# Context products of an expert matrix in one batch ahead of the latents' products, with three split buffer pairs and seven raw buffers

## The chip, the cores and the metric

One core of one Trainium2 chip runs the whole program. The metric is the time on the device in microseconds (us) of one launch, the median over runs.

## What is computed

Two layers over 1024 latent tokens and 256 context tokens of 1024 channels. Each layer has a token mixer and then a mixture of 16 experts in which each expert chooses its tokens: an eighth of the tokens per expert, so 128 latents and, in layer 0 alone, 32 context tokens. The part of the reference that the change touches:

```python
def ec_moe(h, router, w_gate, w_up, w_down):
    cap = CAPACITY_FACTOR * n // N_EXPERTS
    aff = jax.nn.softmax((h @ router).astype(jnp.float32), axis=-1)
    g, idx = lax.top_k(jnp.swapaxes(aff, 1, 2), cap)
    xg = jax.vmap(lambda hb, ib: hb[ib])(h, idx)
    a = jnp.einsum('becd,edf->becf', xg, w_gate)
    u = jnp.einsum('becd,edf->becf', xg, w_up)
    y = jnp.einsum('becf,efd->becd', jax.nn.silu(a) * u, w_down) * g[..., None]
...
x = x + g2 * ec_moe(h_l, ...)
if need_ctx:
    ctx = ctx + cg2 * ec_moe(h_c, ...)
```

Latents and context go through the same three 1024 x 1024 matrices of an expert (gate, up, down), each with its own choice of tokens.

## The kernel before

The program goes through the recurrence of layer 0, its experts (from about 550 to 1365 us of the span), the attention of layer 1, its experts (about 1860 to 2425 us) and the final norm. The change lies in the experts of layer 0.

**Weights.** The 48 expert matrices of a layer come as chunks of 1 MB, four to a matrix, [128 partitions, 2048]: two of the 8 steps of the contraction each. `Stream` issues their loads on SP's queue, in the order of use, into as many raw buffers as its pools have: `raw0` has four, and `rawx` adds one in layer 0. `done(i)` gives the buffer of chunk i back, and `fill` issues the next load into it, which waits for the last readers of the buffer.

**Latents.** A chunk is split into a high part `wh` (a copy on ACT, L209) and a low part `wl` (a subtraction on DVE, L210), both read from the raw chunk. `mm3` (L218, L220, L222) makes one step of the contraction out of six matmuls of 128 x 128 stationary by 512 columns: high by high, high by low, low by high, each for two halves of the 1024 columns. Eight steps make one matrix. `split_upto(k)` issues the splits up to chunk k. It is called at every even step, for AHEAD = 3 chunks past the one in use, and four pairs of `wh` and `wl` take turns: three in the pool `wspA`, one in `wspB` (`Ring`).

**Context.** The 32 context tokens use the raw chunk, unsplit, in fp32. `ctx_mm(c)` puts two steps of the contraction by two halves of the columns side by side on the four column groups of the array: four matmuls of 128 x 32 stationary by 512 columns (L1188), in the profile eight, since each is two instructions. I call these eight a context group. There are four groups to a matrix; `matrix` puts one behind every odd step of the latents, and the chunk's raw buffer is free after it. After the fourth group the result leaves by `joined` (a copy on ACT, L1153, an addition on DVE, L1154), and Silu, the product with the up result or `put` follow. In the very last matrix alone (down of expert 15) all four groups run first and `after_ctx` follows at once, since the context's keys and values are made beside its latents.

**Order.** The order is written by hand: gate(e+1), down(e), up(e+1), and so on; at the end up(15), down(14), down(15). Hooks put small work behind a step: transposes of the activations behind steps 2, 3 and 5 of a gate product (`A_AT`), of the next expert's rows behind steps 3, 4 and 5 of an up product (`X_AT`), each through two PSUM buffers `tp`, and the index matmuls `mt` behind step 6 of a gate product. Names in the profile: `acc` and `accc` are the sums of latents and context, `xh`, `xl`, `ah`, `al` the latents' stationary parts, `xc`, `ac` the context's, `yl`, `yc` the weighted results that POOL adds to `xr` and `xc` in memory by an indirect DMA.

In the loop of a matrix the order is this:

```python
for kt in range(KT):
    k = k0 + kt // 2
    if kt % 2 == 0:
        split_upto(k + AHEAD)
    h, lo = sp[k]
    mm3(acc, side[0][:, kt], side[1][:, kt], h[:, kt % 2], lo[:, kt % 2], D, kt == 0, kt == KT - 1)
    if has_ctx and not after_ctx and kt % 2:
        ctx_mm(kt // 2)
```

Of the kernel before, what the change touches and what calls it, by code (L numbers as in the profile page):

```python
# [9 lines left out]
F32 = mybir.dt.float32  # L10
# [4 lines left out]
OP = mybir.AluOpType  # L15
# [22 lines left out]
class Stream:  # L38
    """Weight chunks of 1 MB, loaded in the order of use as far ahead as buffers allow."""
# [17 lines left out]
    def fill(self, gate=None):  # L57
        """gate: an operation on the buffer that the load has to follow."""
# [34 lines left out]
class Ring:  # L93
    """Four buffers of a tag in turn, three in one pool and one in another."""
# [10 lines left out]
class Parts:  # L105
    """Pools side by side, each of its own tags, so that memory is handed on part by part."""
# [14 lines left out]
def hybrid_kernel(ctx: ExitStack, tc: tile.TileContext, I, out, dbg=None, stop=None):  # L121
# [5 lines left out]
    # ------------------------------------------------------------------ DRAM tables  # L127
# [12 lines left out]
    # ------------------------------------------------------------------ constants  # L140
# [7 lines left out]
    # ------------------------------------------------------------------ weight stream  # L148
# [58 lines left out]
    # ------------------------------------------------------------------ helpers  # L207
# [6 lines left out]
    def mm3(o, h, l, wh, wl, n, start, stop):  # L214
        """o += (h + l)^T (wh + wl) without l^T wl; moving operand cut into banks of 512."""
# [8 lines left out]
    def std_of(pool, ss):  # L224
        """sqrt(ss / D + eps)."""
# [9 lines left out]
    def transpose4(pool, src, c0, tag):  # L235
        """four 128 x 128 transposes of src's columns into one bank."""
# [33 lines left out]
    def ada_steps(l, u, psum, tag, bufs=2):  # L270
        """conditioning unit: 4 groups of 256 columns on 4 column groups of the array; yields after each chunk."""
# [33 lines left out]
    def load_row(pool, name, l, u, row, tag=None):  # L305
        """a row of 1024, the same on every partition."""
# [6 lines left out]
    def route_load(l):  # L313
        """router, and scale and shift of the norm before it, channels on partitions."""
# [9 lines left out]
    # ================================================================== phase 0: norm of the inputs, ada for sh1, sc1  # L324
# [31 lines left out]
    def x_norm(i):  # L356
        """the diagonal of 1 / rms of a tile's tokens."""
# [6 lines left out]
    def x_turn(i):  # L364
        """normalised tokens, channels on partitions."""
# [10 lines left out]
    # ------------------------------------------------------------------ RG-LRU pieces: a block of 128 channels at a time  # L376
# [32 lines left out]
    def mod_cols(half):  # L409
        """1 + scale and shift of four channel tiles, channels on partitions."""  # L410
# [12 lines left out]
    def mod(kts, n):  # L423
        """h = xn (1 + scale) g + shift for one group of tokens, in its two parts."""
# [21 lines left out]
    # log_sigmoid(lam) * 8 = 8 (min(lam, 0) - log1p(exp(-|lam|))), log1p as 2 atanh(y / (2 + y))  # L446
# [80 lines left out]
    # ================================================================== phase 1: RG-LRU  # L527
# [51 lines left out]
    def gates(b, hook=None):  # L579
        """the gates, and the input's gate times the input."""  # L580
# [19 lines left out]
    # a = exp(8 r log_sigmoid(lam)), sqrt(1 - a^2) from tanh(-log a) = (1 - a^2) / (1 + a^2)  # L600
# [44 lines left out]
    # the context's tiles of the output projection: the last two blocks come from the chip  # L645
# [68 lines left out]
    # ================================================================== output projection, residual, norm, router  # L714
# [4 lines left out]
    def out_setup(l, tiles, zpool, get_w, last=None):  # L719
        """tiles: list of (kind, index, first column in ZT[l]); last: parts of the last blocks of ZT, kept on chip."""  # L720
# [1392 lines left out]
```

## Time and profile before

| | |
|---|---|
| median of 3 runs | 2467.14 us (2462.00 to 2470.66) |
| span of the profiled execution, first to last instruction | 2461.8 us |
| its own time | not listed apart from the three runs |
| mean granted TensorE clock | 0.975 of full speed |
| busy: PE / PEld / DVE / ACT / POOL | 95% / 70% / 74% / 58% / 14% |
| chain that ended last | PE 73%, issue 9%, DVE 7%, ACT 5%, DMA 4% |
| moved by DMA | 607.55 MB, 247 GB/s mean |

The profile is of one execution. A busy PE says that matmul records overlap without a gap, not that the array streams at its peak: the time that a change of the array's use costs is found between the starts of neighbouring matmuls. The median of the runs lies 5.3 us above the span, the lowest run 0.2 us.

### The profile page before, as it was taken

What the parts mean: (1) busy time and instruction counts of PE and PEld (TensorE: products, weight loads), DVE (VectorE), ACT (ScalarE), POOL (GpSimd) and SP (SyncE); (2) the same over time, 40 slices, a digit from 0 to 9 for tenths busy, and PEclk for the clock granted to TensorE, in tenths of its full rate; (3) what the DMA queues carried; (4) which work ended last, traced back from release to release, by engine and by line L of the source; (5) the groups of instructions that cost most, each with busy time, mean ns of one, the idle gap of its engine ahead of it and who ended that gap; (6) DMA issues with size and microseconds to landing.
All of it is one profiled execution on the core that took longest, in us unless ns stands there. A gap on an engine that the chain in (4) does not pass through costs nothing.

```text
span 2461.8 us, 32211 instructions
## 1 busy us (share of the span) xinstructions
PE 2341.2 (95%) x12693; PEld 1721.7 (70%) x12693; DVE 1832.2 (74%) x2239; ACT 1438.4 (58%) x1524; POOL 338.1 (14%) x299
## 2 busy tenths in 40 slices
PE   7999998969999999999999899999967999999998
PEld 6778877746656566666565688787746888888885
DVE  6578787567777777777776654886476999999997
ACT  5667784326555655555555422786235777777775
POOL 0001002112121111211110211023220110111010
PEclk9999999979999999999999999999988999999999
DMA  8444336457788788877877622223856999999994
GB/s 332 173 154 164 133 129 239 154 199 275 277 269 297 269 279 276 277 277 267 288 263 271 210 79 81 92 69 132 298 205 225 383 377 389 382 378 392 380 378 157
DMA packets 106615, 607.55 MB, mean 247 GB/s; under 512 B 13872, under 2 KB 15616, under 8 KB 48352
## 3 DMA queue, kind: packets, MB, share of 16 engines
q1 hardware_dynamic: 73024, 494.67, 53.4%
q0 software_dynamic: 31424, 107.35, 14.6%
q10 hardware_dynamic: 2016, 3.48, 0.5%
q8 instruction: 100, 1.64, 0.3%
q14 instruction: 51, 0.42, 0.1%
HBM read 549.39 MB, written 56.05 MB: 246 GB/s over the span
## 4 chain that ended last, share of the span: by engine, by line
PE 73%; issue 9%; DVE 7%; ACT 5%; DMA 4%; POOL 1%; SPq 0%; POOLq 0%; ACTq 0%; DVEq 0%
PE acc L218 15%; PE acc L222 14%; PE acc L220 14%; PE accc L1188 6%; PE psx L398 4%; PE psy L398 4%; PE tp L239 3%; PE gps L591 2%; PE u L222 1%; PE u L218 1%; PE u L220 1%; PE ada L282 1%; ACT pth L209 1%; ACT pm L1759 1%; DMA xr<-yl,ixl 1%
## 5 line engine op out<-in xcount | busy, mean ns | idle before, releaser
L210 DVE TENSOR_TENSOR wl<-raw,wh 128x2048 fp32r<-128x2048 f32 x382 | 870.0, 2288 | 267.1 <-ACT wh L209 262.7
L209 ACT ACTIVATE wh<-raw 128x2048 fp32r<-128x2048 f32 (+1 forms) x392 | 741.4, 1897 | 341.3 <-DMA raw<-in_moe_w 244.4
L218 PE MATMUL acc<-wh,xh 128*128 128x512 f32 x1056 | 354.8, 417 | 0.0
L222 PE MATMUL acc<-wh,xl 128*128 128x512 f32 x1056 | 333.1, 396 | 0.0
L220 PE MATMUL acc<-wl,xh 128*128 128x512 f32 x1056 | 332.4, 396 | 0.0
L218 PEld LDWEIGHTS acc<-wh,xh 128*128 128x128 f32 x1056 | 180.9, 190 | 83.6 <-issue 46.9
L222 PEld LDWEIGHTS acc<-wh,xl 128*128 128x128 f32 x1056 | 199.0, 188 | 47.6
L220 PEld LDWEIGHTS acc<-wl,xh 128*128 128x128 f32 x1056 | 199.0, 188 | 47.1
L218 PE MATMUL acc<-wh,ah 128*128 128x512 f32 x480 | 155.3, 405 | 0.0
L220 PE MATMUL acc<-wl,ah 128*128 128x512 f32 x480 | 148.7, 391 | 0.0
L222 PE MATMUL acc<-wh,al 128*128 128x512 f32 x480 | 148.3, 390 | 0.0
L1249 POOL DMA_INDIRECT xr<-yl,ixl x31 | 109.1, 3520 | 231.4 <-DVE yl L1248 183.1
L1188 PE MATMUL accc<-raw,xc 128*32 128x512 f32 x1024 | 136.4, 605 | 0.0
L218 PEld LDWEIGHTS acc<-wh,ah 128*128 128x128 f32 x480 | 85.2, 188 | 63.2 <-issue 41.9
L1120 POOL DMA_INDIRECT xgl<-hl,ixl x32 | 31.9, 998 | 664.6 <-DVE ixc L1115 319.0
L220 PEld LDWEIGHTS acc<-wl,ah 128*128 128x128 f32 x480 | 90.1, 188 | 19.7
L222 PEld LDWEIGHTS acc<-wh,al 128*128 128x128 f32 x480 | 90.1, 188 | 19.6
L209 ACT ACTIVATE xh<-tp 128x512 fp32r<-128x512 f32 x72 | 42.6, 593 | 90.5 <-PE tp L239 77.2
L218 PE MATMUL u<-wqh,hah 128*128 128x512 f32 x192 | 76.9, 400 | 0.2 <-ACT hah L209 0.2
L222 PE MATMUL u<-wqh,hal 128*128 128x512 f32 x192 | 75.2, 391 | 0.0
L220 PE MATMUL u<-wql,hah 128*128 128x512 f32 x192 | 74.8, 390 | 0.0
L1188 PE MATMUL accc<-raw,ac 128*32 128x512 f32 x512 | 67.4, 604 | 0.0
(497 smaller groups left out, 4137.5 us busy)
## 6 DMA issues: line engine op xcount, KB each, us to landing
raw<-in_moe_w SPq DMA_DIRECT2D x384, 1024.0 KB, 7.3
raw<-in_ada_w SPq DMA_DIRECT2D x48, 1024.0 KB, 7.6
raw<-in_w_in SPq DMA_DIRECT2D x8, 1024.0 KB, 6.2
xr<-xres POOLq DMA_DIRECT2D x16, 512.0 KB, 3.9
hl<-h POOLq DMA_DIRECT2D x16, 512.0 KB, 2.9
raw<-in_xall SPq DMA_DIRECT2D x6, 1024.0 KB, 6.7
raw<-in_w_qkv SPq DMA_DIRECT2D x6, 1024.0 KB, 7.5
zt<-y POOLq DMA_DIRECT2D x7, 640.0 KB, 4.1
```

The costliest lines, as they stand in the source:

```text
L209: ACT.activation(h, src, AF.Copy)
L210: low_on[0].tensor_tensor(l, src, h.bitcast(F32), OP.subtract)
L218: PE.matmul(o[:, a:b], h, wh[:, a:b], start=start, stop=False)
L220: PE.matmul(o[:, a:b], h, wl[:, a:b], start=False, stop=False)
L222: PE.matmul(o[:, a:b], l, wh[:, a:b], start=False, stop=stop)
L239: PE.transpose(tp[:, q * P:(q + 1) * P], src[:, c0 + q * P:c0 + (q + 1) * P], ident)
L282: PE.matmul(ps[32 * j:32 * j + 32, 0:256], scol[:, kt, :], w[:, q * 1024 + j * 256:q * 1024 + (j + 1) * 256], start=(kt == 0), stop=(kt == ...
L398: PE.matmul(ps[:, n, 0:b - a], w_[:, kt], x_[:, kt, a:b], start=f_, stop=e_)
L591: PE.matmul(ps[:, n, 0:b_ - a], wt[:, c0:c0 + P], s[xt][:, a:b_], start=f, stop=e)
L1120: POOL.indirect_dma_start(out=t, out_offset=None, in_=rowsrc[kd], in_offset=bass.IndirectOffsetOnAxis(ap=ix[:, :1], axis=0))
L1188: PE.matmul(accc[32 * j:32 * j + 32], side_c[2 * c + r], w[:, r * D + n * 512:r * D + (n + 1) * 512], start=c == 0, stop=c == 3)
L1249: POOL.indirect_dma_start(out=rowdst[kd], out_offset=bass.IndirectOffsetOnAxis(ap=ix[:, :1], axis=0), in_=t, in_offset=None, compute_op=OP ...
```

## The change

In layer 0 all four context groups of a matrix run in one batch at the start of the matrix, ahead of its latents' steps, as only the last matrix did before. What follows from the context's sum is issued before step 1 of the latents. A raw chunk is free when both its split and its context group have been issued (`half_done` counts the two). The splits use three pairs (`wspA` alone) and run two chunks ahead; the two buffers of `wspB` become raw buffers of the stream, for chunks before the last matrix: 4 + 1 + 2 = 7. Comments and docstrings are also taken out, so line numbers move by a few. The core of the diff:

```diff
+    halves = set()
+    def half_done(i):
+        if i in halves:
+            st.done(i)
+        halves.add(i)
...
-                pool, nb = (wspl, 4) if l == 0 else (wspA, 3)
-                h = pool.tile([P, 2, D], F32R, name="wh", tag="wh", bufs=nb)
-                lo = pool.tile([P, 2, D], F32R, name="wl", tag="wl", bufs=nb)
+                h = wspA.tile([P, 2, D], F32R, name="wh", tag="wh", bufs=3)
+                lo = wspA.tile([P, 2, D], F32R, name="wl", tag="wl", bufs=3)
                 split(h, lo, w.rearrange("p (a b) -> p a b", a=2))
                 sp[kk] = (h, lo)
                 if l == 1:
                     st.done(i)
+                else:
+                    half_done(i)
...
-        AHEAD = 3 if l == 0 else 2
+        AHEAD = 2
...
+            split_upto(k0 + AHEAD - 1)
+            if has_ctx:
+                accc = ps.tile([P, 512], F32, name="accc", tag="accc", bufs=2)
+                for c, i in enumerate(ids[("moe", l, e, m)]):
+                    w = st.get(i)
+                    for j in range(4):
+                        r, n = j // 2, j % 2
+                        PE.matmul(accc[32 * j:32 * j + 32], side_c[2 * c + r],
+                                  w[:, r * D + n * 512:r * D + (n + 1) * 512], start=c == 0, stop=c == 3)
+                for i in ids[("moe", l, e, m)]:
+                    half_done(i)
             for kt in range(KT):
                 k = k0 + kt // 2
                 if kt % 2 == 0:
                     split_upto(k + AHEAD)
+                if has_ctx and kt == 1:
+                    after_ctx(accc)
                 h, lo = sp[k]
                 mm3(acc, side[0][:, kt], side[1][:, kt], h[:, kt % 2], lo[:, kt % 2], D, kt == 0, kt == KT - 1)
-                if has_ctx and not after_ctx and kt % 2:
-                    ctx_mm(kt // 2)
...
+            for t in ("wh", "wl"):
+                st.add_pool(wspB, 1, ids[("moe", l, NE - 1, 2)][0], t)
...
+        st.drop_pool(wspB)
...
+    wspl.n = {"wh": 2, "wl": 2}
```

`gate_mm`, `up_mm` and `down_mm` hand what they did with the context's sum after the matrix to `matrix` as `after_ctx`; what it computes is the same. The last line sets the ring so that the first split of the attention's weights, made beside down(15), uses `wspB`.

How the instructions move. TensorE (PE), from the end of gate(4) into down(3), before; the number at a name's end tells buffers apart:

```order
L1188 MATMUL accc_5873<-raw109_5835,xc_5840 32x512 x4
L218 MATMUL acc_6026<-wh_5900,ah_5870 128x512 x2
L220 MATMUL acc_6026<-wl_5901,ah_5870 128x512 x2
L222 MATMUL acc_6026<-wh_5900,al_5871 128x512 x2
L218 MATMUL acc_6026<-wh_5900,ah_5870 128x512 x2
L220 MATMUL acc_6026<-wl_5901,ah_5870 128x512 x2
L222 MATMUL acc_6026<-wh_5900,al_5871 128x512 x2
L1188 MATMUL accc_6027<-raw110_5862,ac_5963 32x512 x4
L218 MATMUL acc_6026<-wh_5936,ah_5870 128x512 x2
L220 MATMUL acc_6026<-wl_5937,ah_5870 128x512 x2
L222 MATMUL acc_6026<-wh_5936,al_5871 128x512 x2
```

The same place in the change:

```order
L218 MATMUL acc_5874<-wh_5922,xh_5755 128x512 x2
L220 MATMUL acc_5874<-wl_5923,xh_5755 128x512 x2
L222 MATMUL acc_5874<-wh_5922,xl_5756 128x512 x2
L1198 MATMUL accc_6029<-raw110_5777,ac_5975 32x512 x4
L1198 MATMUL accc_6029<-raw111_5783,ac_5975 32x512 x4
L1198 MATMUL accc_6029<-raw112_5805,ac_5975 32x512 x4
L1198 MATMUL accc_6029<-raw113_5892,ac_5975 32x512 x4
L218 MATMUL acc_6028<-wh_5954,ah_5872 128x512 x2
L220 MATMUL acc_6028<-wl_5955,ah_5872 128x512 x2
L222 MATMUL acc_6028<-wh_5954,al_5873 128x512 x2
L218 MATMUL acc_6028<-wh_5954,ah_5872 128x512 x2
```

The four context groups (`accc`, x4 matmuls each) stand together between two matrices; behind the odd steps there is none any more.

ScalarE (ACT) at the same matrix, chunks raw110 to raw113, before; the copies `wh` are the splits, `sgc` and `yc` the context's results of gate(4) and down(3):

```order
L1221 ACTIVATE sg_6020<-acc_5872 128x1024
L1153 ACTIVATE sgc_6022<-accc_5873 64x512
L1226 ACTIVATE sgc_6022<-sgc_6022 64x512
L209 ACTIVATE wh_6028<-raw113_5956 128x2048
L209 ACTIVATE wh_6050<-raw114_6018 128x2048
L209 ACTIVATE wh_6072<-raw115_6048 128x2048
L209 ACTIVATE wh_6094<-raw116_6070 128x2048
L1153 ACTIVATE yc_6116<-accc_6027 64x512
L209 ACTIVATE wh_6128<-raw117_6092 128x2048
```

And in the change:

```order
L209 ACTIVATE wh_5954<-raw110_5777 128x2048
L1156 ACTIVATE ac_5975<-tpc_5970 128x256
L209 ACTIVATE wh_5977<-raw111_5783 128x2048
L1226 ACTIVATE sg_6026<-acc_5874 128x1024
L209 ACTIVATE wh_6050<-raw112_5805 128x2048
L1161 ACTIVATE yc_6062<-accc_6029 64x512
L209 ACTIVATE wh_6073<-raw113_5892 128x2048
L209 ACTIVATE wh_6091<-raw114_5894 128x2048
```

At the start of down(3) (after `sg`, the Silu of gate(4)) the split now due is of chunk raw112, two past the first in use; before it was raw113. The copy of down(3)'s context result stands behind that split, where it stood behind that of raw116.

## Rows read from the trace of the kernel before

**Rows 1.** the page's part 1, busy time of each engine over the span
```profile
PE 2341.2 (95%) x12693; PEld 1721.7 (70%) x12693; DVE 1832.2 (74%) x2239; ACT 1438.4 (58%) x1524; POOL 338.1 (14%) x299
```

**Rows 2.** busy time by stretch: length, engines (xcount), PE clock, DMA share, GB/s
```profile
600.00:1300.00 700.00, 698.81 (x3756) 422.18 (x3755) 507.08 (x470) 397.33 (x317) 105.48 (x58) 1.00 0.81 277
1365.00:1380.00 15.00, 7.70 (x29) 6.40 (x29) 10.45 (x12) 8.05 (x12) 2.76 (x3) 0.66 0.78 262
1870.00:2370.00 500.00, 500.00 (x2359) 406.88 (x2358) 457.56 (x321) 364.09 (x241) 57.72 (x27) 1.00 0.99 378
```

**Rows 3.** all waits of PE from 558 to 1365 us: total, times, longest
```profile
PE tp L239 <- DVE a L1232: 3.3, 2, 2.1
```

**Rows 4.** PE timeline, latent steps of down(6) beside a context group: start, length
```profile
912.89 0.62 PE L222 MATMUL acc<-wh,al 128*128 128x512 f32 x2
913.35 0.62 PE L218 MATMUL acc<-wh,ah 128*128 128x512 f32 x2
...
914.26 0.61 PE L222 MATMUL acc<-wh,al 128*128 128x512 f32 x2
914.81 1.06 PE L1188 MATMUL accc<-raw,ac 128*32 128x512 f32 x8
915.80 0.73 PE L218 MATMUL acc<-wh,ah 128*128 128x512 f32 x2
916.37 0.63 PE L220 MATMUL acc<-wl,ah 128*128 128x512 f32 x2
```

**Rows 5.** PE timeline, gate(7), steps with transposes after them
```profile
899.09 0.62 PE L222 MATMUL acc<-wh,xl 128*128 128x512 f32 x2
899.55 0.60 PE L239 MATMUL tp<-ident,a 128*128 128x128 f32 x4
899.91 0.71 PE L218 MATMUL acc<-wh,xh 128*128 128x512 f32 x2
...
900.93 0.63 PE L222 MATMUL acc<-wh,xl 128*128 128x512 f32 x2
901.49 1.06 PE L1188 MATMUL accc<-raw,xc 128*32 128x512 f32 x8
902.48 0.66 PE L239 MATMUL tp<-ident,a 128*128 128x128 f32 x4
902.89 0.71 PE L218 MATMUL acc<-wh,xh 128*128 128x512 f32 x2
```

**Rows 6.** PE timeline, the last down product: five context groups in one run
```profile
1348.79 4.50 PE L1188 MATMUL accc<-raw,ac 128*32 128x512 f32 x40
1353.22 0.72 PE L218 MATMUL acc<-wh,xh 128*128 128x512 f32 x2
```

**Rows 7.** groups by line, 560 to 1360 us: busy, mean ns, idle before
```profile
L210 DVE TENSOR_TENSOR wl<-raw,wh 128x2048 fp32r<-128x2048 f32 x190 | 433.4, 2288 | 213.5 <-ACT wh L209 210.9 <-PE accc L1188 2.2
L209 ACT ACTIVATE wh<-raw 128x2048 fp32r<-128x2048 f32 x188 | 359.1, 1913 | 230.9 <-DMA raw<-in_moe_w 222.8 <-DVE wl L210 4.5 <-DVE yc L1248 1.3
...
L1188 PEld LDWEIGHTS accc<-raw,xc 128*32 128x32 f32 x1016 | 20.0, 108 | 46.5 <-issue 45.7 <-ACT wh L209 0.7
...
L210 DVE TENSOR_TENSOR al<-tp,ah 128x512 fp32r<-128x512 f32 x30 | 19.2, 680 | 0.0
```

**Rows 8.** ACT timeline from 908 us, the Silu at the end of gate(7)
```profile
910.97 1.02 ACT L1221 ACTIVATE sg<-acc 128x1024 f32<-128x1024 f32 x1 [1.43 <-PE acc L222]
```

**Rows 9.** DMA issues, 600 to 1290 us: count, KB each, us to landing
```profile
raw<-in_moe_w SPq DMA_DIRECT2D x164, 1024.0 KB, 6.1
```

**Rows 10.** the chain of waits, 676 to 695 us: start, us, what
```profile
681.79 10.14 DMA raw<-in_moe_w
```

**Rows 11.** the chain of waits, 1345 to 1380 us
```profile
1361.69 7.62 DMA xc<-xc
```

**Rows 12.** all waits of PE from 1295 to 1400 us
```profile
PE tp L239 <- DVE xc L1447: 4.4, 1, 4.4
PE tp L239 <- DVE xl L210: 3.2, 1, 3.2
```

More of the change, by code (lines that the diff above doesn't have):

```diff
@@ L1173, in moe @@
         pos_in, sp, split_upto = ms or moe_split(l)
-        AHEAD = 3 if l == 0 else 2
+        AHEAD = 2
         def matrix(m, e, side, side_c, hooks, after_ctx=None):
             acc = ps.tile([P, D], F32, name="acc", tag="acc", bufs=2)
-            accc = ps.tile([P, 512], F32, name="accc", tag="accc", bufs=2) if has_ctx else None
             k0 = pos_in[m, e, 0]
-            def ctx_mm(c):
-                i = ids[("moe", l, e, m)][c]
-                w = st.get(i)
-                for j in range(4):
-                    r, n = j // 2, j % 2
-                    PE.matmul(accc[32 * j:32 * j + 32], side_c[2 * c + r], w[:, r * D + n * 512:r * D + (n + 1) * 512],
-                              start=c == 0, stop=c == 3)
-                if not (after_ctx and c == 3):
-                    st.done(i)
-            dead = []
-            if after_ctx:
-                split_upto(k0 + AHEAD - 1)
-                for c in range(4):
-                    ctx_mm(c)
-                after_ctx(accc)
-                split_upto(k0 + AHEAD)
-                st.done(ids[("moe", l, e, m)][3])
+            split_upto(k0 + AHEAD - 1)
[9 more added lines that the diff above has]
+                    half_done(i)
             for kt in range(KT):
@@ L1204, in matrix @@
                     split_upto(k + AHEAD)
+                if has_ctx and kt == 1:
+                    after_ctx(accc)
                 h, lo = sp[k]
                 mm3(acc, side[0][:, kt], side[1][:, kt], h[:, kt % 2], lo[:, kt % 2], D, kt == 0, kt == KT - 1)
[L1207 to L1210 removed]
                 if kt == KT - 1:
[L1212 removed]
+                    for k2 in range(k0, k0 + 4):
                         sp.pop(k2)
@@ L1215, in matrix, with after_c @@
                     f()
-            return acc, accc
+            return acc
         def gate_mm(e, hooks):
-            a, ac = matrix(0, e, X["l", e], X.get(("c", e)), hooks)
-            sg = p.tile([P, D], F32, name="sg", tag="sg", bufs=1)
-            ACT.activation(sg, a, AF.Silu)
-            SG["l", e] = sg
-            if has_ctx:
+            def after_c(ac):
                 sc_ = p.tile([64, 512], F32, name="sgc", tag="sgc", bufs=1)
@@ L1227, in gate_mm, with after_c @@
                 SG["c", e] = sc_
+            a = matrix(0, e, X["l", e], X.get(("c", e)), hooks, after_c)
+            sg = p.tile([P, D], F32, name="sg", tag="sg", bufs=1)
+            ACT.activation(sg, a, AF.Silu)
+            SG["l", e] = sg
         def up_mm(e, hooks):
-            u, uc = matrix(1, e, X.pop(("l", e)), X.pop(("c", e), None), hooks)
-            a = p.tile([P, D], F32, name="a", tag="a", bufs=1)
-            DVE.tensor_tensor(a, SG.pop(("l", e)), u, OP.mult)
-            Act["l", e] = a
-            if has_ctx:
+            def after_c(uc):
                 a = p.tile([64, 512], F32, name="acx", tag="acx", bufs=1)
@@ L1238, in up_mm @@
                 Act["c", e] = a
+            u = matrix(1, e, X.pop(("l", e)), X.pop(("c", e), None), hooks, after_c)
+            a = p.tile([P, D], F32, name="a", tag="a", bufs=1)
+            DVE.tensor_tensor(a, SG.pop(("l", e)), u, OP.mult)
+            Act["l", e] = a
         def put(kd, e, src):
@@ L1252, in down_mm @@
         def down_mm(e, hooks, after_ctx=None, use=None):
-            y, yc = matrix(2, e, Act.pop(("l", e)), Act.pop(("c", e), None), hooks, after_ctx)
+            y = matrix(2, e, Act.pop(("l", e)), Act.pop(("c", e), None), hooks,
+                       after_ctx or (lambda yc: put("c", e, yc)))
             if use:
                 return use(y)
-            if has_ctx and not after_ctx:
-                put("c", e, yc)
             put("l", e, y)
```

3 lines of the change are left out of this document (removed).

## The prediction

> **What bounds the kernel now.** I read the busy times first: PE 95% of the span, DVE 74%, ACT 58% [rows 1]. That average covers many stages, so next the table by stretch: in the experts of layer 0 PE is busy for 698.81 of 700 us at the full clock of 2.4 GHz (granted clock 1.00), while DVE has 507.08, ACT 397.33 and DMA moves 277 GB/s; in the experts of layer 1 DMA moves 378 GB/s over 500 us [rows 2]. So in layer 0 PE is the bound, and DMA has room. The list of PE's waits confirms it: 3.3 us in all, two waits, over the stage [rows 3]. A busy PE need not be an efficient one, so the last view is the timeline, and there the starts of neighbouring matmuls, not the modelled ends.
>
> Two matmuls of the latents take 0.46 us from start to start (912.89 to 913.35), so six, one step, 1.4 us. A context group between two latent steps costs more than its own time, in three places [rows 4]. **Entry**: from the last pair ahead of the group to the group 0.55 us (914.26 to 914.81), 0.09 above 0.46. **The group**: 0.99 us to the next matmul (914.81 to 915.80). **Re-entry**: the first pair after it takes 0.57 us (915.80 to 916.37), 0.11 above 0.46.
>
> What a group costs where it follows another one shows once, at the end: five groups in a run (the last one of down(14) and the four of down(15), 40 instructions) take 1353.22 - 1348.79 = 4.43 us [rows 6]. If the last, which is followed by latents, takes 0.99, the other four take 3.44, so 0.86 each. The exit costs 0.13.
>
> **PE's sum.** Today there are 188 visits to the context's groups: four in each of 47 matrices, the 47th boundary visit running on into the batch of the last matrix. In the change there are 48, one ahead of each matrix. The 47 visits behind step 7 stand in the same place as a batch, so what goes are the three behind steps 1, 3 and 5, 141 in all, and one comes, ahead of the first matrix. The 192 groups themselves stay.
>
> A plain visit gives back 0.09 + 0.13 + 0.11 = 0.33 us. Where a transpose follows the group, the transposes themselves remain and have a cost of their own: after latents they start 0.46 after the last pair (899.09 to 899.55) and last 0.36 to the next matmul; after a group the entry is 0.56 (900.93 to 901.49) and they last 0.41 (902.48 to 902.89) [rows 5]. Such a visit gives back 0.10 + 0.13 + 0.05 = 0.28. These are the visits behind steps 3 and 5 of 15 gates, 15 ups and down(14): 62. Then 79 x 0.33 + 62 x 0.28 = 26.1 + 17.4 = 43.5 us, less 0.3 for the new visit: **43.1 us**, 0.9 per matrix.
>
> Here a page speaks against the change. In this kernel a batch is only better inside than apart if weight loads hide behind the group ahead; they are 32 columns by 128 rows and take 108 ns each [rows 7], and the run of five shows 0.86 per group with them in it [rows 6]. The Trainium skill, "TensorE: Matmul & The Clock Gate", Part 3 (what overlaps and what doesn't), says that a weight load overlaps with running matmuls only when its row group differs, and all of these have the same rows; its description of the mechanism also allows a background weight buffer. By the first sentence alone the exit's 0.13 would not be saved. The row decides for 0.86, and the other case is a rival below.
>
> **The splits.** With three pairs the split of chunk k+3 can start when PE has left chunk k, and must be done two chunks later, where four pairs gave three. Its price: 1.91 us on ACT, then 2.29 on DVE [rows 7], 4.2 in a row. Two chunks are four steps, 5.6 us. Let 0 be the batch's start; latents start at 0.09 + 3.44 + 0.1 = 3.6. The third chunk's pair comes free at 0 and is needed at 3.6 + 5.6 = 9.2; with Silu of the gate (1.02 us [rows 8]) ahead of it on ACT it is done at about 5.5. The fourth chunk's pair is free at 6.4 and the split done at 10.8; step 6 is at 12. The next matrix's first two have its batch as well. Least slack: in a gate the transposes behind step 5 reuse the first `tp` buffer, which is free when DVE has done the fourth chunk's split and one piece of 0.68 us [rows 7], about 11.5, and stand at 13: 1.5 us. Behind the context's addition on DVE, ACT's Silu waits, and behind it ACT's next split; DVE's addition follows the third chunk's split at once and works on 64 x 512, half of what the Silu above does per partition; both are past by the 6.4. So I cost the three pairs at 0 (at worst 1 us in the 31 gates and ups with transposes, the upper end).
>
> **The loads.** A raw buffer is held until split and batch are past. Per matrix two loads are issued at the batch's end (3.6), one behind the third chunk's split, one behind the fourth's (about 11). The tightest load is the fourth chunk of the next matrix, issued at 3.6; the batch needs it at 15 + 2.6: 14 us later. A load lands in 6.1 us (median), in one case in 10.1 [rows 9, 10]. SP's queue has only these loads here. At 4 MB per matrix in 0.9 us less the rate goes to about 293 GB/s, still below the 378 of layer 1 [rows 2]. Cost 0. Both waits of PE (3.3 us) come behind a late load: with 5 buffers the split came late, held up DVE's product `a` behind it, and the transposes waited for that. With two buffers more they should go: **-3.3 us** against this execution (between 0 and 3.3).
>
> **The end of layer 0.** In the last matrix the batch stays where it is, but the first load of the attention's weights now waits for chunk 188 to have both its split and its batch, as the fourth chunk's split stands behind that weight's split on ACT. Landing in 5 to 6 us after 3.6, then 1.9 and 1.9 on ACT and 2.3 on DVE: the low part is there at about 15.5, where step 6 stands at 12. So the latents end some 3 us later, counted from the batch. That is covered: PE waits 4.4 us there for the context's rows, and 3.2 for the second tile [rows 12], at 0.66 of the clock [rows 2]. These rows come sooner by about 1 us, since the put of expert 14 is long past, and the second tile's load (7.62 us, [rows 11]) no longer meets the weights' loads, which are 3 us later. I take **-2 us**, between +3 (cover gone) and -6.
>
> **Sum:** 43.1 + 3.3 + 2 = 48.4 us. Against the profiled execution 2461.8 becomes 2413.4. Its span is 5.3 below the median of the runs, what lies around it included; against the median, 2467.1 - 48.4 = **2418.7 us**, 2.0% faster.
>
> **Rivals.**
> - *Loads show in the batch* (no exit saved): 79 x 0.20 + 62 x 0.15 = 25.1 instead of 43.5, so 2437. Against it the run of five; for it only that it is one run. 4%.
> - *Three pairs bind.* 1 us in each of 31 matrices of those with transposes is lost, 31 us: 2450. For it the slack of 1.5 us, which is an estimate from ends of 4 instructions; against it the batch, which gives 3.5 us in each matrix. 7%.
> - *Slower: the batch waits for its fourth chunk.* Today a late chunk delays only its own step; a batch stops PE as a whole. It decides when a load lands later than 14 us after its issue, and loses more than is won when 1.2 us past that (54 us over 47). With the slow landing of 10.1 [rows 10] as the rule and the three loads behind one another at 2.7 us each (1 MB at 378 GB/s), 18 us, each matrix would wait 4 us: 188 - 48, 2607. Against it: the median of 6.1, and no two slow ones in a row are seen. 2%.
> - *Nothing moves*, since the visits are hidden by something else: 2467. PE's full row and its missing waits speak against it [rows 2, 3]. 2%.
>
> **Chances.** The forecast has 85%; 0.3% (7.4 us) is about what a measurement can tell from no change. Faster by more: 0.95 with the first two rivals; within: 0.02; slower: 0.03. The range takes the forecast with the waits' and the end's bounds (2418.7 - 4 for the end, + 3.3 + 5 for them) and the spread of the runs (4 to 5 us), and the first rival: 2408 to 2438.
>
> **What would show it.** PE's timeline: 32 instructions in a run of about 3.4 us ahead of each matrix, eight latent steps with no break but the transposes, and a period some 0.9 to 1 us shorter. The table by stretch: PE still full between 600 and 1250, DMA near 293 GB/s. PE's waits: none for `wh`, `wl`, `tp` or a load. If waits of `acc` for `wl` or of `tp` for `al` show up in gates, the second rival is right; if the groups in the batch start 0.99 apart, the first; if `accc` waits for DMA, the third. Layer 1 should keep its length.

## The result and the profile after

The changed kernel takes **2422.66 us** (median of 4 runs, 2420.98 to 2423.64) against 2466.39 us of the kernel before in the same session: a ratio of 0.9826, 95% interval 0.981 to 0.9843. The forecast was 2418.7 us, the range 2408 to 2438. The profiled execution took 2423.64 us, its span is 2421.6 us: 40.2 less than the span before.

The page's part 1, busy time of each engine over the span:

```profile
PE 2300.1 (95%) x12693; PEld 1747.6 (72%) x12693; DVE 1833.6 (76%) x2241; ACT 1438.1 (59%) x1524; POOL 350.0 (14%) x299
```

PE has the same number of instructions as before [rows 1] and is as full as before, but 41 us shorter: what was removed did not show as idle time. Busy time by stretch (length, PE, PEld, DVE, ACT, POOL, granted clock, DMA share, GB/s): the experts of layer 0, the end of that stage, the experts of layer 1.

```profile
600.00:1260.00 660.00, 660.00 (x3759) 442.67 (x3761) 512.82 (x474) 400.53 (x317) 119.47 (x58) 1.00 0.82 293
1325.00:1340.00 15.00, 8.45 (x29) 6.73 (x29) 11.34 (x13) 8.93 (x13) 3.73 (x3) 0.55 0.55 155
1830.00:2330.00 500.00, 500.00 (x2359) 406.91 (x2358) 457.43 (x321) 364.72 (x241) 57.67 (x27) 1.00 1.00 379
```

PE does 3759 matmuls in 660 us of the first stretch, where 700 us held 3756 [rows 2]; the DMA rate went to 293 GB/s, and layer 1 is as it was. PE's waits from 545 to 1345 us (total, times, longest):

```profile
PE tp L239 <- DVE xc L1451: 9.3, 1, 9.3
PE tp L239 <- DMA xgl<-hl,ixl: 5.7, 1, 5.7
PE tp L239 <- DVE xl L210: 2.4, 1, 2.4
PE tpc L1154 <- DVE xl L210: 0.6, 1, 0.6
...
```

The second and fourth stand ahead of the first matrix, as before. Inside the stage no wait is left (before: 3.3 us, [rows 3]). But the wait at the end for the context's rows, 4.4 us before [rows 12], has become 9.3.

The timeline of PE where one matrix ends and the next begins (start, length):

```profile
619.60 0.62 PE L220 MATMUL acc<-wl,ah 128*128 128x512 f32 x2
620.05 0.61 PE L222 MATMUL acc<-wh,al 128*128 128x512 f32 x2
620.60 3.64 PE L1198 MATMUL accc<-raw,xc 128*32 128x512 f32 x32
624.17 0.72 PE L218 MATMUL acc<-wh,xh 128*128 128x512 f32 x2
624.73 0.63 PE L220 MATMUL acc<-wl,xh 128*128 128x512 f32 x2
```

The batch of 32 instructions takes 3.57 us to the next matmul of the latents, four groups where one took 0.99 [rows 4]. Entry (620.05 to 620.60) takes 0.55 us and re-entry (624.17 to 624.73) 0.56, as large as before, but paid once a matrix.

Where the time went, between milestones of the two profiled executions (starts of PE's matmuls in the trace):

| stretch | before | after | change |
|---|---|---|---|
| first to last matmul of the experts of layer 0 | 810.65 | 764.77 | -45.9 |
| from there to the first keys' product `ukv` | 11.58 | 15.69 | +4.1 |
| attention, first `u` to the first scores | 146.11 | 146.11 | 0 |
| experts of layer 1 | 570.00 | 570.68 | +0.7 |

### The profile page after: what moved, and what is told of

It reads as the page before. It is cut to its first block, busy times and chain, and to the rows that moved or that the text cites. A ratio compares the mean times of both kernels' runs of the same rounds, so it can differ in the third digit from the quotient of the medians.

```text
span 2421.6 us, 32195 instructions
## 1 busy us (share of the span) xinstructions
PE 2300.1 (95%) x12693; PEld 1747.6 (72%) x12693; DVE 1833.6 (76%) x2241; ACT 1438.1 (59%) x1524; POOL 350.0 (14%) x299
## 3 DMA queue, kind: packets, MB, share of 16 engines
q0 software_dynamic: 31424, 107.35, 14.6%
## 4 chain that ended last, share of the span: by engine, by line
PE 77%; issue 7%; DVE 7%; ACT 5%; DMA 3%; POOL 1%; SPq 0%; POOLq 0%; ACTq 0%; DVEq 0%
PE acc L218 16%; PE acc L222 15%; PE acc L220 15%; PE accc L1198 6%; PE psx L398 4%; PE psy L398 4%; PE tp L239 3%; PE gps L591 2%; PE ada L282 2%; PE u L222 1%; PE u L218 1%; PE u L220 1%; ACT pth L209 1%; PE s L1742 1%; ACT pm L1763 1%
## 5 line engine op out<-in xcount | busy, mean ns | idle before, releaser
L1250 POOL DMA_INDIRECT xr<-yl,ixl x31 | 102.4, 3302 | 374.1 <-DVE yl L1249 318.1
L218 PE MATMUL acc<-wh,ah 128*128 128x512 f32 x480 | 150.2, 394 | 0.0
L1198 PE MATMUL accc<-raw,xc 128*32 128x512 f32 x1024 | 119.3, 607 | 0.0
L1198 PEld LDWEIGHTS accc<-raw,xc 128*32 128x32 f32 x1024 | 30.6, 111 | 70.6 <-issue 70.6
```

The lines of the kernel that those rows point to most:

```text
L218: PE.matmul(o[:, a:b], h, wh[:, a:b], start=start, stop=False)
L1198: PE.matmul(accc[32 * j:32 * j + 32], side_c[2 * c + r], w[:, r * D + n * 512:r * D + (n + 1) * 512], start=c == 0, stop=c == 3)
L1250: POOL.indirect_dma_start(out=rowdst[kd], out_offset=bass.IndirectOffsetOnAxis(ap=ix[:, :1], axis=0), in_=t, in_offset=None, compute_op=OP ...
```

## The experiments

"Period" below is the time from the first latents' matmul of a matrix to that of the next, from the starts in the trace (medians); apart from the first matrix, the last few and late loads, matrices of a kind lie within 0.05 us of each other, far closer than the totals do. "The tail" is the time from the last product of the experts of layer 0 to the first `ukv`. The kernel before ran again beside each group of runs, with medians of 2464.1 to 2466.4 us, and each ratio is to the runs beside. The two medians of the changed kernel lie 3.4 us apart, so smaller differences between rows are read from the trace.

| run | median us | ratio to the kernel before, 95% | period down / up / gate | tail |
|---|---|---|---|---|
| kernel before | 2465.2 | 1 | 15.79 / 16.91 / 17.80 | 11.58 |
| changed kernel | 2422.66 | 0.981 to 0.9843 | 14.68 / 16.04 / 17.05 | 15.69 |
| batch, old buffers | 2422.62 | 0.9813 to 0.9846 | 14.68 / 16.04 / 17.05 | 16.55 |
| new buffers, old order | 2464.62 | 0.9989 to 1.0009 | 15.79 / 16.91 / 17.80 | 18.06 |
| two visits | 2435.98 | 0.987 to 0.9903 | 15.10 / 16.36 / 17.38 | 16.54 |
| late weights | 2417.90 | 0.9795 to 0.9828 | 14.68 / 16.04 / 17.05 | 11.72 |
| three pairs, five raw | 2419.19 | 0.9799 to 0.9829 | 14.68 / 16.04 / 17.05 | 16.27 |
| merged transposes | 2419.22 | 0.9798 to 0.9832 | 14.68 / 16.01 / 17.03 | 11.61 |
| context transposes at the batch | 2416.67 | 0.9791 to 0.9818 | 14.68 / 16.43 / 16.47 | 12.07 |
| weights behind rows | 2417.77 | 0.9788 to 0.9822 | as above | 16.47 |
| rows first | 2415.06 | 0.9772 to 0.9804 | as above | 13.29 |
| latents' put last | 2413.12 | 0.9783 to 0.981 | as above | 9.37 |
| changed kernel again | 2419.26 | 0.9806 to 0.9833 | 14.68 / 16.04 / 17.05 | 15.35 |

### Which part of the change gained: the order or the buffers

**Batch, old buffers**: four pairs, three chunks ahead, five raw buffers, with the batch.

```diff
-                h = wspA.tile([P, 2, D], F32R, name="wh", tag="wh", bufs=3)
+                pool, nb = (wspl, 4) if l == 0 else (wspA, 3)
+                h = pool.tile([P, 2, D], F32R, name="wh", tag="wh", bufs=nb)
...
-        AHEAD = 2
+        AHEAD = 3 if l == 0 else 2
...
-            for t in ("wh", "wl"):
-                st.add_pool(wspB, 1, ids[("moe", l, NE - 1, 2)][0], t)
```

> The batch alone: all four groups of context products ahead of the latents' products, but the buffers of the kernel before (four split pairs, three steps ahead, five raw buffers, none lent to the stream). A raw buffer is still given back by whichever comes second, its split or its group. Theory 1 (the gain is the visits of the column groups alone, 141 of them at some 0.33 us, and buffers cost and give nothing): same as the changed kernel, 2420 to 2426 us, the stage of the experts of layer 0 764 to 768 us. Theory 2 (the batch needs four raw buffers of a matrix at once, so that five are too few, and the last chunk of a matrix lands late): the batch waits for its fourth chunk, by the landing of 7 us that a load takes less the lead it has; a wait of 1 to 3 us a matrix over 48 matrices gives 2470 to 2570 us, and the waits show as accc<-raw,ac with a DMA as releaser.

Measured: 2422.62 us, the changed kernel's time, and its periods to 0.01 us. **New buffers, old order** is the other half: three pairs and seven raw buffers, each group behind its own step.

```diff
+                if has_ctx and not whole and kt % 2:
+                    groups((kt // 2,))
```

> The buffers alone: three split pairs and seven raw buffers as in the changed kernel, but each group of context products behind its own step of the latents again (four visits a matrix, only the last matrix of the layer in a batch, as before). Theory 1 (visits): the time of the kernel before, 2463 to 2470 us, at most 3 us less where the late loads' waits of the kernel before [rows 3] are gone. Rival (the extra raw buffers are what gained, by earlier loads): most of the 44 us stays, 2420 to 2435 us. Rival (three pairs bind when the latents' steps have no batch between matrices): slower than before, 2470 to 2490 us, with waits of TensorE on splits.

Measured: 2464.62 us, ratio 0.9999, the periods of the kernel before. So the order alone carries the gain, and the buffers give nothing to the total: its stage is 4.9 us shorter than before (805.78; the two late loads are gone, and the clock rose sooner at its start), its tail 6.5 us longer, of which more below. **Three pairs, five raw** takes the extra buffers out of the changed kernel.

```diff
-            for t in ("wh", "wl"):
-                st.add_pool(wspB, 1, ids[("moe", l, NE - 1, 2)][0], t)
```

> The changed kernel without the two extra raw buffers: three split pairs, five raw buffers, so that less is loaded ahead than in any of the kernels so far. Theory 1 (loads have enough lead even with five): 2420 to 2426 us, the same period of 14.68, 16.04 and 17.05 us for the three kinds of matrix. Theory 2 (the seven buffers are what the three pairs and the batch live on): waits of TensorE for a raw chunk ahead of the batch or for splits; 1 us in each of 47 matrices would give some 2470 us.

Measured: 2419.19 us and the same periods; theory 1, with a total 0.8 us below its range. PE's waits for it, 545 to 1345 us, have none for a chunk or a split of the experts:

```profile
PE tp L239 <- DVE xc L1448: 9.9, 1, 9.9
PE tp L239 <- DMA xgl<-hl,ixl: 5.6, 1, 5.6
PE tp L239 <- DVE xl L210: 2.4, 1, 2.4
PE tpc L1154 <- DVE xl L210: 0.6, 1, 0.6
...
```

### Is it the number of visits

**Two visits** a matrix: groups 0 and 1 ahead of it, 2 and 3 behind the second step.

```diff
+                groups(range(4) if whole else (0, 1))
...
+                if has_ctx and not whole and kt == 1:
+                    groups((2, 3))
```

> A dose between: groups 0 and 1 of a matrix ahead of its first step, groups 2 and 3 behind its second row of products, so two visits a matrix and not one (47 of the 48 matrices; the last one stays whole); buffers as in the changed kernel. Theory 1 (each visit has a price of its own, some 0.33 us plain): 47 x 0.33 = 15.5 us above the changed kernel, 2436 to 2441 us. Rival (what gains is that the context's products are ahead of the latents' and cover the late chunk, not the number of visits): within 4 us of the changed kernel, 2420 to 2427 us. The visit in the middle should show, start to start, 0.55 us at its entry-to-first-group step and about 1.0 us for its last group.

Measured: 2435.98 us, the lower end of theory 1; on the stage, 780.38 - 764.77 = 15.6 us for 47 visits, **0.33 us a visit**. The start of the stage hides a little more: two groups of the first matrix run at the lower clock here and four in the changed kernel, which is worth 1.2 us. By the periods, free of that, a visit costs an up or a gate 0.33 us and a down 0.41. One of its visits in PE's timeline, between a down and the up behind it:

```profile
910.94 0.61 PE L222 MATMUL acc<-wh,al 128*128 128x512 f32 x2
911.49 1.92 PE L1198 MATMUL accc<-raw,xc 128*32 128x512 f32 x16
913.34 0.74 PE L218 MATMUL acc<-wh,xh 128*128 128x512 f32 x2
913.92 0.62 PE L220 MATMUL acc<-wl,xh 128*128 128x512 f32 x2
```

The price does not depend on the length. Medians over 15 or 16 matrices, in us, between the starts of single matmuls (last latents to first group; first group to next latents; that one to its neighbour); the price is their sum less two undisturbed steps of 0.232 and 0.858 a group, which is (3.571 - 0.996) / 3:

| groups in a visit | entry | to next latents | re-entry | price |
|---|---|---|---|---|
| 1 (old order) | 0.318 | 0.996 | 0.337 | 0.33 |
| 2 (two visits) | 0.318 | 1.854 | 0.341 | 0.33 |
| 4 (changed kernel) | 0.318 | 3.571 | 0.335 | 0.33 |

### What the price is for

Two runs on top of the late weights (next section), whose stage is the changed kernel's, 764.74 us. **Merged transposes** puts the two sets of four 128 x 128 transposes behind the same step.

```diff
-A_AT = (2, 3, 5)
-X_AT = (3, 4, 5)
+A_AT = (2, 2, 5)
+X_AT = (3, 3, 5)
```

> Another kind of visit, on top of the late weights of the experiment before: the two sets of four 128 x 128 transposes of the latents, which stood behind two different steps of a gate's and an up's products, stand behind one and the same step, in 31 matrices of layer 0 (and of layer 1 likewise). Theory 1 (the price belongs to groups that use a part of the array, 32 columns or 64 rows; whole-array transposes have no entry step of their own, and what their re-entry costs, 0.08 us, they win back at the last of the four, which is left 0.08 us early): no change, 2416 to 2420 us, gate and up keep 17.05 and 16.04 us. Rival (every break in a run of latents' products costs some 0.33 us, whatever it is): 31 x 0.33 = 10 us less, 2406 to 2410 us. Against both: the two sets need two splits in a row on ScalarE and VectorE, and where that holds up the weights' split, TensorE waits.

Measured: the stage 764.10 us, 0.6 less than with late weights alone, for 31 visits fewer; the totals, 2419.22 and 2417.90, show no gain either. So breaking the run of the latents is not by itself what costs. **Context transposes at the batch** moves the small transposes of the context's activations from the middle of a gate to the end of the up before it.

```diff
-                steps.append(c_)
+                hooks.setdefault(7, []).append(c_)
...
-                up_mm(e + 1, place_at(X_AT, prep_x(e + 2)))
+                up_mm(e + 1, with_ac(e + 1, place_at(X_AT, prep_x(e + 2))))
```

> On top of the late weights: the four 64 x 64 transposes of the context's activations, which stood alone behind the sixth step of a gate's products, move to the end of the up before it, where the next gate's batch of context groups follows at once. They stand 0.33 us behind the last matmul of the latents and the matmul after them is followed 0.34 us later, as at a visit of groups. Theory 1 (the price is for a change between the whole array and parts of it, and parts of different shape share one visit): entry 0.10, exit about 0.09 and re-entry 0.11 us go 15 times, some 4 to 4.5 us less, 2412 to 2415 us, the gate's period 16.75 and the up's unchanged but for the transposes' own 0.25 us. Rival (a change between two part shapes costs as much as one between whole and part): no change, 2416 to 2420 us.

PE's timeline in the changed kernel, where these transposes stand alone:

```profile
935.68 0.64 PE L222 MATMUL acc<-wh,xl 128*128 128x512 f32 x2
936.24 0.46 PE L1154 MATMUL tpc<-ident,acx 64*128 64x64 f32 x4
936.63 0.73 PE L218 MATMUL acc<-wh,xh 128*128 128x512 f32 x2
937.20 0.64 PE L220 MATMUL acc<-wl,xh 128*128 128x512 f32 x2
```

And at the batch:

```profile
918.88 0.63 PE L222 MATMUL acc<-wh,xl 128*128 128x512 f32 x2
919.44 0.46 PE L1154 MATMUL tpc<-ident,acx 64*128 64x64 f32 x4
919.83 3.64 PE L1201 MATMUL accc<-raw,xc 128*32 128x512 f32 x32
923.40 0.73 PE L218 MATMUL acc<-wh,xh 128*128 128x512 f32 x2
```

Alone they have an entry of 0.56 after the last pair and a re-entry of 0.57, like a visit of groups; whole-array transposes enter at 0.46 [rows 5]. At the batch one entry and one re-entry serve both. Up and gate together fall from 33.09 to 32.90 us, 0.19 a pair, and the stage from 764.74 to 761.55: **3.2 us**, between theory 1 (4 to 4.5) and its rival (0). What stays is the step between the two shapes: 0.39 from the first transpose to the first group, as much as to a latents' matmul. By the total (2416.67 against 2417.90) this can't be told.

### The tail

**Late weights**: the gates of the three weight loads (memsets of a raw buffer on VectorE, L1058, which each load has to follow) behind the context's first norm.

```diff
-        hooks = {1: [lambda: wq_split(0, wspl, 4, (0,))], 3: [lambda: more(4)], 7: [lambda: norm(0)]}
+        hooks = {1: [lambda: wq_split(0, wspl, 4, (0,))], 7: [lambda: norm(0), lambda: more(4)]}
```

> The tail of layer 0 alone: the three gates that let the loads of the query, key and value weights go (the memsets of raw buffers on VectorE) move from behind the fourth row of the last matrix's products to its end, so that the rows of the context's tokens are read back ahead of them; all else as in the changed kernel. Theory A (the 4 us that the tail got longer are the row loads' landing, 7.6 us behind 3 MB of weights): the first tile lands in some 4 us as before, TensorE's wait of 9.3 us before the first transposes falls to 5 to 6 us, 2418 to 2420 us. Theory B (the wait is set by the scatter of the context's sums and its landing, and by a load that takes 7 us with or without weights beside it): no change at the wait, 2422 to 2424 us. If the weights are then late for the keys' products, the wait comes back in front of those and the time is 2422 us or more.

Measured: tail 11.72 us, PE's wait 5.3, the time 2417.90: theory A. The timelines of DVE, POOL, SP's queue and ACT around the rows' load `xc<-xc`; first the kernel before:

```profile
1361.12 1.16 POOL L1486 DMA_DIRECT2D xc<-xc  x2 [3.02 <-DMA xc<-yc,iy]
1361.75 0.07 DVE L1058 MEMSET raw<- 128x1 f32 x3
1361.96 1.31 SPq L69 DMA_DIRECT2D raw<-in_w_qkv  x3
1364.72 1.06 ACT L1444 ACTIVATE junk<-xc 128x1024 f32<-128x1024 f32 x1 [5.65 <-DMA xc<-xc]
```

The changed kernel:

```profile
1316.80 0.08 DVE L1058 MEMSET raw<- 128x1 f32 x3
1316.89 1.16 POOL L1490 DMA_DIRECT2D xc<-xc  x2 [4.06 <-DMA xc<-yc,iy]
1317.03 1.32 SPq L69 DMA_DIRECT2D raw<-in_w_qkv  x3
1324.51 1.06 ACT L1448 ACTIVATE junk<-xc 128x1024 f32<-128x1024 f32 x1 [10.38 <-DMA xc<-xc]
```

Late weights:

```profile
1314.88 1.16 POOL L1490 DMA_DIRECT2D xc<-xc  x2 [3.99 <-DMA xc<-yc,iy]
1318.57 1.06 ACT L1448 ACTIVATE junk<-xc 128x1024 f32<-128x1024 f32 x1 [6.29 <-DMA xc<-xc]
...
1322.99 2.63 SPq L69 DMA_DIRECT2D raw<-in_w_qkv  x3
```

ACT's square is the first to read the rows. From the issue to it: 3.60 us where the weights follow 0.84 us later, 7.62 us where they follow 0.14 us later. The late weights cost something behind: from the first `ukv` to the first scores 16.42 + 147.33 us, against 15.63 + 146.11.

The last three runs stand on top of the context transposes at the batch. **Weights behind rows** takes the gates ahead of the norm again, at the end of the matrix.

```diff
-7: [lambda: norm(0), lambda: more(4)]}
+7: [lambda: more(4), lambda: norm(0)]}
```

> On top of the context transposes at the batch: the gates of the three weight loads move from behind the context's first norm to ahead of it, at the end of the last matrix's products, so that the loads are let go right behind the issue of the rows' loads (the rows' load was issued at 1314.88 us in the run with late weights, VectorE's last split ended at 1315.0) and not 8 us after it. With the gates behind the norm, the stretch from the first keys' product to the scores took 147.33 + 16.42 us and with the transposes at the batch 149.32 + 17.64 us, against 146.11 + 15.63 in the changed kernel: late weights gave back 2 to 5 us there. Theory A (it is only the order of issue that counts: rows ahead of the weights): first tile's load 4 to 5 us, TensorE's wait 5 to 6 us, and the 146.1 + 15.6 us come back, 2411 to 2414 us. Theory B (the loads share the engines however close behind they come): the rows take 6 us or more, the wait grows by 2 us or more, 2414 to 2417 us.

Measured: 2417.77 us, a miss. The weights' gate came 0.37 us ahead of the rows, not behind them:

```profile
1308.77 0.08 DVE L1058 MEMSET raw<- 128x1 f32 x3
1308.99 1.32 SPq L69 DMA_DIRECT2D raw<-in_w_qkv  x3
1309.14 1.16 POOL L1493 DMA_DIRECT2D xc<-xc  x2 [4.48 <-DMA xc<-yc,iy]
1317.17 1.06 ACT L1451 ACTIVATE junk<-xc 128x1024 f32<-128x1024 f32 x1 [11.08 <-DMA xc<-xc]
```

The rows took 8.03 us. The edit did not bring about the order it was to test, so it does not decide between the two theories; that the loads share the engines, as theory B says, is seen in the packets ("What was not expected of the hardware"). The stretch behind came back to 15.59 + 146.18 us.

**Rows first** does the last context sums ahead of the third chunk's split, and their scatter ahead of that of the latents of expert 14.

```diff
+                if has_ctx and last and kt == 0:
+                    after_ctx(accc)
                 if kt % 2 == 0:
                     split_upto(k + AHEAD)
...
             put("c", NE - 1, yc)
+            put("l", NE - 2, late.pop())
```

> The same, and the context's sums of the last expert go first: VectorE's and ScalarE's work on them stands ahead of the split of the last matrix's third chunk, their scatter ahead of that of the latents of expert 14, and the split of the first query, key and value weight three steps later. In the run with late weights the split of that chunk held VectorE until 1307.70 us while the sums were ready for it at 1306.93, and the latents' scatter held GpSimd from 1305.79 to 1309.18; the context's scatter started at 1309.48. Expected: scatter 0.8 to 1 us sooner, counted from the batch's start, so the rows' load and TensorE's wait 0.8 to 1 us shorter, 1 us below the run beside it (less than the totals can tell; it is read from the time from the last product of the experts to the first keys' product). Rival: the splits of the last two chunks come too late, TensorE waits 1 to 3 us inside the last matrix, and nothing or less than nothing is left.

Measured: 2415.06 us, tail 13.29 against 16.47: more than expected, since the weights now follow 3.7 us behind the rows. Still the rows take 7.1 us:

```profile
1305.13 1.45 POOL L1257 DMA_INDIRECT xc<-yc,iy  x1 [13.97 <-DVE yc L1256]
1306.88 3.56 POOL L1257 DMA_INDIRECT xr<-yl,ixl  x1 [0.30 <-issue]
1309.86 1.77 POOL L1501 DMA_DIRECT2D xc<-xc  x2
...
1313.56 1.49 SPq L69 DMA_DIRECT2D raw<-in_w_qkv  x3
1316.97 1.06 ACT L1458 ACTIVATE junk<-xc 128x1024 f32<-128x1024 f32 x1 [6.69 <-DMA xc<-xc]
```

**Latents' put last** moves that scatter behind the rows' loads.

```diff
             put("c", NE - 1, yc)
-            put("l", NE - 2, late.pop())
...
                 POOL.dma_start(X[i], XC[i * P:(i + 1) * P])
+            put("l", NE - 2, late.pop())
```

> As the run before it, but the scatter of the latents of expert 14 stands behind the loads of the context's rows in GpSimd's queue. There the rows were let go at 1309.86 us, 3.5 us ahead of the weights, and still took 7 us to land: 512 KB of the latents' scatter, from 1306.88 to 1310.44, had been issued right ahead of them. Theory A (the rows waited for what was ahead of them, first the weights and then the scatter): the load lands in some 4 us, TensorE's wait of 6.9 us falls to 3 to 4 us, from the last product of the experts to the first keys' product 10 us in place of 13.3, the time 2411 to 2413 us. Theory B (a rows' load takes 7 us whatever stands ahead): 13 us, 2414 to 2417 us. If the scatter is then late for the first latents' tile of the attention, the 15.6 or the 146.1 us behind it grow.

```profile
1308.84 1.17 POOL L1500 DMA_DIRECT2D xc<-xc  x2 [2.85 <-DMA xc<-yc,iy]
1310.31 1.83 POOL L1257 DMA_INDIRECT xr<-yl,ixl  x1 [0.30 <-issue]
1312.46 1.06 ACT L1458 ACTIVATE junk<-xc 128x1024 f32<-128x1024 f32 x1 [2.77 <-DMA xc<-xc]
...
1312.97 1.49 SPq L69 DMA_DIRECT2D raw<-in_w_qkv  x3
```

Measured: 3.62 us from issue to use, PE's wait 3.0, tail 9.37: theory A. The time is **2413.12 us** (2410.84 to 2415.97), and the changed kernel beside it on the same chip:

> The changed kernel again, beside the last one on the same chip, so that the two can be compared by runs of one hour: 2420 to 2425 us.

2419.26 us (2417.19 to 2420.04). The two sets of runs do not overlap: 6.1 us, 0.25%. This version beats both kernels, and the changed kernel's own tail is where the larger part of it was: 15.35 - 9.37 = 6.0 us, beside 2.6 on the stage. The spans of the two profiled executions differ by 5.0 only: with the latents' put last the stage began 1.6 us later, and from the first `ukv` on the rest took 2.0 more.

## Why the prediction was right, and which step was not

**The mechanism and the size of the main term: right.** The sum had -43.1 us for 141 visits and -3.3 for late loads, -46.4 on the stage; measured were -45.9. The order alone (new buffers, old order, against the changed kernel) is 805.78 - 764.77 = 41.0 us. In the changed kernel the first batch ran at the lower level of the clock, 6.4 us instead of 3.57; in the other run three pairs of the latents did, 0.85 us each and not 0.46, 1.2 us. Without that the visits are worth 41.0 + 2.8 - 1.2 = 42.6. That this lies so near to 43.1 is in part luck, since the errors by kind, next, offset one another.

**The prices by kind were off in both directions.** The same two runs differ by 15.5 us in the first 14 downs, 13.2 in 15 ups and 11.2 in 15 gates, where the prices of 0.33 and 0.28 give 13.9, 13.4 and 13.4. In a gate, the prediction priced the transposes behind step 5 like whole-array ones; they are the context's, 64 x 64. They shared the visit's entry, and now stand alone. The run with these transposes at the batch gives 3.2 us back. In a down, the other matmuls of the latents, too, stand a little closer in the changed kernel: 0.2274 us on average against 0.2298. Why, no run tells.

**A page and the exit.** In the batch every group but the last costs 0.858 with its weight loads inside, as the run of five groups in the kernel before said [rows 6]. In the trace the loads of a batch run beside its matmuls (at 621.05 us four loads of 0.11 us, and four matmuls that last until 621.66). The rule of the Trainium skill that was weighed against it, in "TensorE: Matmul & The Clock Gate", Part 3, that a load overlaps only where its row group differs, is not borne out here: all loads have the same rows, and the exit's 0.13 us was saved.

**The late loads: right in size, wrong in cause.** Both waits went: the matrices that held them have periods shorter by 1.40 and 2.31 us, 3.7 in all. But they went in the batch with five raw buffers as well. So it is not the two extra buffers that the batch needed; the runs do not tell why the two loads were late in that one execution.

**Three pairs cost 0, the loads cost 0: right.** Four pairs or three, five raw buffers or seven, the periods are the same to 0.01 us, although the median landing of a chunk between 600 and 1290 us went from 6.1 us before [rows 9] to 7.0 in the changed kernel and 8.1 in the batch with old buffers. None of this is on PE's path. One step of the working was wrong without harm: the text had the first weight's load wait for the whole batch, 3.6 us. SP issued it at 1305.69, 1.1 us after the batch began at 1304.57: the buffer was free as soon as PE had passed its chunk's own group. So the latents did not end 3 us later either: their last matmul starts 14.6 us after the batch in both kernels.

**The end of layer 0: wrong.** The step said that the rows come 1 us sooner and that their second tile no longer meets the weights' loads, -2 us, between -6 and +3. Measured: +4.1. Counted from the start of the last batch (1349.67 before, the second of the five groups; 1304.57 after), the weights' gate stayed at 12.1 and 12.2 us, while the rows' load slipped from 11.4 to 12.3. That the gate would stay where it was, and the rows would not come sooner, the text did not see; a shift of 0.7 us in the order of two issues cost 4 us of landing. The rows wait for the context's scatter, and the step "the put of expert 14 is long past" failed: that holds for the context's put, not for the latents', which GpSimd issues right ahead of it on the same queue:

```profile
1307.73 3.38 POOL L1250 DMA_INDIRECT xr<-yl,ixl  x1 [11.36 <-DVE yl L1249]
1311.42 1.42 POOL L1250 DMA_INDIRECT xc<-yc,iy  x1 [0.30 <-issue]
```

The context's scatter itself started 0.2 us sooner than before but landed in 4.92 us, not 3.88, in both kernels 0.6 to 0.7 us after the latents' scatter; with that one behind it, as with rows first and with the latents' put last, it landed in 3.75. The latents' scatter landed later than before, 11.1 us after the batch's start against 10.3: GpSimd took 3.38 us to issue it, 1.60 before. What held GpSimd, no run tests. The range held, since the main term did.

**The total.** -45.9 and +4.1, beside +1.6 in small differences of the other stages, make the 40.2 us between the two spans. The span before was at the low end of its runs, so the medians lie 43.7 us apart.

## What to carry to other kernels

A busy engine is not a full one: look at the starts of neighbouring matmuls on both sides of each change of instruction shape, and count the changes rather than the work. Here 0.33 us a visit, invisible as idle time, was 1.7% of the kernel, and it was won by order alone, with no buffer more. Whoever shifts a stage by a few us should then list, for the next stage's first load, what is issued just ahead of it on every queue: 0.7 us in the order of two issues gave back a tenth of the gain.

## What was not expected of the hardware

- **The change of array shape costs, the break does not.** PE's groups of 32 columns and transposes of 64 rows enter 0.09 to 0.10 us late and the latents behind them come 0.11 late; transposes of the whole array enter on time, and merging 31 of them gained 0.6 us. The Trainium skill, "TensorEngine Tiling (Array Packing)", Key Properties, says that a change of tiling mode drains TensorE; the rows agree, and put 0.33 us on going there and back, at 8, 16 or 32 instructions.
- **A load's landing depended on what was issued beside it, also on another queue.** From issue to use, the first tile of the rows (512 KB) took 3.60 us with 3 MB of weights 0.84 us behind it (3.69 at 8.1 us, 3.62 at 4.1), 7.62 at 0.14 us behind, 8.03 with the weights 0.15 us ahead, 8.26 and 8.32 at 1.5 us ahead. The packets of the two queues, first of the kernel before from 1362.3 to 1364.2 us, then of the changed kernel from 1320.1 to 1323.7 (packets, MB, share of the engines; q0 is GpSimd's queue, q1 is SP's):

```profile
q0 software_dynamic: 154, 0.57, 93.6%
...
q1 hardware_dynamic: 138, 1.00, 66.2%
q0 software_dynamic: 134, 0.52, 35.4%
```

  The first tile is 128 packets of 4 KB, a chunk of weights 128 of 8 KB (the counts above hold packets of 4 bytes too, and the first line the start of the second tile). Before, the tile's first packet started 1.3 us after the issue and the 128 took 1.7 us, done before the weights' first packet at 1364.29. In the changed kernel the first started 3.2 us after the issue, when 79 packets of the weights had started, and the 128 took 3.5 us with 115 packets of the weights among them, 1 MB beside 0.5. So the rows stand not behind all of the weights but in turn with them, and the longer packets get two thirds of the bytes. The Trainium skill, "DMA: Bandwidth & Descriptors", Queues, rings and completion order, has an engine take turns between queues packet by packet; the trace agrees. Why the first packet starts 1.9 us later, no run tells.
- **The first work of the stage ran at the lower clock, a batch as well as latents.** Before the first batch PE waits 5.7 us for its rows; the batch then ran at a granted clock of 0.50, 1.2 GHz, and took 6.4 us. By stretch, as above, in the changed kernel:

```profile
556.00:560.00 4.00, 4.00 (x24) 1.13 (x20) 3.83 (x12) 1.64 (x1) 0.99 (x2) 0.50 0.91 352
560.00:564.00 4.00, 4.00 (x22) 2.60 (x15) 3.09 (x4) 2.53 (x4) 4.00 (x3) 0.98 0.99 411
```

  When it rises differs by execution: in the changed kernel's second run the same batch took 4.89 us, and the first matrix of the old order 19.00 us in one run and 17.82 in the other. In these two pairs that is 1.5 and 1.2 us of the totals.
